# Hybrid encoder layer: the MLP in two phases, with the down projection as seven half-size products

## The chip, the cores and the metric

The kernel runs on one NeuronCore of a Trainium2 chip. The metric is the device time of one execution in microseconds. The kernel before took 2099.94 us, the median of three runs (2098.85 to 2100.46). Its profile comes from one more execution, which has a time of its own (below).

All data are float32. TensorE gets every large operand as two parts of the type fp32r, a high part and the rest, and adds three matmuls (high x high, high x low, low x high), so that close to float32 accuracy is kept.

## The reference

One layer on 512 tokens of width 2048. Two mixers read the normalised input, their outputs are projected and added to the residual, then comes a gated MLP of width 5632 with a convolution of width 3 over the tokens, and a last RMS norm:

```python
proj = jnp.einsum("bsd,dc->bsc", rms_norm(x, attn_norm_g), w_in)      # 2048 -> 5120
y_conv = conformer_conv(u_val, u_gate, ...)                           # first two column blocks
y_na = neighborhood_attention(q, k, v, rpb)                           # other three column blocks
mixed = jnp.concatenate([rms_norm(y_conv, conv_out_g), rms_norm(y_na, na_out_g)], axis=-1)
x = x + jnp.einsum("bsc,cd->bsd", mixed, w_out)                       # 2048 -> 2048
up = jnp.einsum("bsd,df->bsf", rms_norm(x, ffn_norm_g), w_up)         # 2048 -> 2 x 5632
up = depthwise_conv(up, ffn_dw_w, ffn_dw_b)                           # width 3, over tokens
gate, val = jnp.split(up, 2, axis=-1)
x = x + jnp.einsum("bsf,fd->bsd", jax.nn.silu(gate) * val, w_down)    # 5632 -> 2048
return rms_norm(x, final_norm_g)
```

The change concerns the MLP and the last norm, and what the stages ahead of them carry for these two.

## The kernel before

**Layout.** Activations are held with channels on the 128 partitions and the 512 tokens along the free axis: 16 tiles for the width of 2048 (KD), 44 for the hidden width (NF). Weights come from DRAM in units of 128 x 1024 (512 KB), eight 128 x 128 blocks each. A block is stationary in TensorE and an activation tile moves past it.

**The weight pipeline.** `raw_unit` (L103) loads a unit on SP's queue into one of 7 raw buffers (NR). `parts` (L107) splits it: ACT writes the high part `whi` (L110), VectorE the low part `wlo` (L111), each in one of 4 buffers (NW). `plan` lists in order how every unit of the program is made, and `weights()` (L142) hands out the next one. Each call first makes the units up to 3 places ahead (AHEAD), so that their loads and splits stand in the engines' queues before the matmuls that use them; and it starts the entries of `sums` up to 8 places ahead (FAR). `mm3` (L118 to L123) issues the three matmuls of a block: L121 high x high, L122 high weight x low activation, L123 low weight x high activation. `tick` lets statistics and attention steps advance between units.

**The stages.** The projections, with convolution and attention beside them, run to about 500 us. The output projection follows in two halves (`out_half`, L461), the convolution group's to about 612 us, the attention group's to about 699 us. `after` (L501) closes each of the 16 column tiles of the second half: it adds the product to the residual x2 (L503), writes the sum to DRAM (`xd`), adds its squares, and for each pair of tiles makes seven combinations for the up projection.

**The up projection.** It is done by the Strassen-Winograd scheme: the 2 x 2 block product (a pair of width tiles by two halves of 256 tokens; gate and value columns) needs seven products of half the size in place of eight. The activations' seven combinations are made once (`comb`, through `halves`, L494 to L499: a split of 128 x 256 by ACT L497 and VectorE L498). The weights' combinations are made anew for each of the 44 hidden tiles in `factors` (L535): the quarters A22, A11 and A12 are used as they are, the sums A22 + A21 and A21 + A11 are made by an accumulating DMA of POOL's queue on a raw buffer (L543), the other two by VectorE adds (L554, L560). `up` (L597) runs the products in the order 0 to 6, each of 8 blocks x 3 matmuls, 256 wide; it copies products 0, 1 and 3 out of PSUM by ACT and joins the rest by VectorE adds. `hidden` (L641) multiplies gate and value by the norm's factor (L643, L644), convolves each (`conv3`: ACT L635, VectorE L636 and L637), and forms silu(gate) x value (L646, L647).

**The down projection** runs beside it, a chunk of 4 hidden tiles (CH) behind: 11 chunks (NCH). When a chunk's four tiles are made, `in_two` splits them. While the next chunk's up products run, `down` (L656) issues 4 x 3 matmuls, 512 wide, for each of the 16 output tiles, copies the result out of PSUM (L665), and adds it to the residual in DRAM with an accumulating DMA on POOL's queue (L666). `down_units` sets after which up products this happens. At the last chunk the residual is loaded back, and the last down products run in two halves of 256 tokens (L700 to L712). Each half's norm takes the sum of squares over the partitions by matmuls (L177, L193), and `finish` (L696) applies norm and gain (L697) and writes the output, channel tile by channel tile (L698). The host transposes it.

**What orders the work.** Every engine, and each DMA queue (SP's and POOL's), runs its instructions in the order in which the program emits them, with few exceptions (`issue_after`, `keep_in_program_order`, `shifted`). An instruction that waits holds up all that stand behind it in its queue.

Of the kernel before, what the change touches and what calls it, by code (L numbers as in the profile page):

```python
# [16 lines left out]
P = 128  # L17
# [17 lines left out]
U = 8  # L35
# [6 lines left out]
CH = 4  # L42
NCH = NF // CH
# [6 lines left out]

ORDER = "aaaqqaqaaaqqaqqq"
# [4 lines left out]
         ("nag", NC_), ("g2", KD), ("fww", 2 * NF * 3), ("fwb", 2 * NF), ("g3", KD)]  # L56
# [9 lines left out]
def layer(ctx: ExitStack, tc: tile.TileContext, xT, w_in, w_out, w_up, w_down, par, tab, out):  # L66
# [51 lines left out]
    def mm3(ps, w, wk, mh, ml, start, stop):  # L118
        hi, lo = w[:2]
        a = slice(wk * P, (wk + 1) * P)  # L120
        nc.tensor.matmul(ps, hi[:, a], mh, start=start, stop=False)  # L121
        nc.tensor.matmul(ps, hi[:, a], ml, start=False, stop=False)  # L122
        return nc.tensor.matmul(ps, lo[:, a], mh, start=False, stop=stop)  # L123
# [18 lines left out]
    def weights():  # L142
        at = weights.at
        weights.at += 1
        for i in range(at, min(at + 1 + FAR, len(plan))):
            sum_ = sums.pop(i, None)
            if sum_ is not None:
                sum_()
# [3 lines left out]

    sums = {}

    weights.at = 0
# [94 lines left out]
    def project(n):  # L250
        ps = psm.tile([P, S], F32, tag="mm", name="pj")
        for u in range(KD // U):
# [4 lines left out]
            tick(m)  # L257
            while late:
                late.pop()()
# [201 lines left out]
    def out_half(m, read):  # L461
        for d in range(KD):
# [4 lines left out]
            tick(i)  # L467
            read(d, ps)
# [22 lines left out]
    xd = [dram.tile([P, S], F32, name=f"x2d{d}") for d in range(KD)]  # L491
# [8 lines left out]

    def after(d, ps):  # L501

        nc.vector.tensor_add(x2[d], x2[d], ps)  # L503
        nc.sync.dma_start(xd[d], x2[d])
        sum_sq(acc2, x2[d], d == 0)
        if d % 2 == 0:
            return
# [14 lines left out]
        for c, f in enumerate((t4_, t1, t3, b11, t2_, b21, b22)):  # L522
            halves(f, c)
# [11 lines left out]
    def factors(f):  # L535
# [5 lines left out]
        def summed(q1, q2):  # L541
            t = load(q1)
            nc.gpsimd.dma_start(t, w_up[f, q2], accum_op=ALU.add)  # L543
            return t

        def make(c):
            if c == 0:
                return load(A22)
            if c == 1:
                return a["s"]  # L550
            elif c == 2:
                return a[A21]
            elif c == 3:
                return load(A11)  # L554
            elif c == 4:
                add(a["s"], a["s"], a[A11])
            elif c == 5:
                return load(A12)
            else:
                add(a["s"], a["s"], a[A12])  # L560
            return a["s"]

        a = {}

        def ahead(c):
# [211 lines left out]
```

## Time and profile before

| | before |
|---|---|
| median of three runs | 2099.94 us (2098.85 to 2100.46) |
| the profiled execution's own time | 2099.91 us |
| its span, first to last instruction | 2098.1 us |
| matmuls / TensorE's mean granted clock | 13024 / 0.995 of full speed |
| moved by DMA | 340 MB, on average 162 GB/s |

How to read it. The page gives each engine's busy time as a share of the span: PE is TensorE's matmuls, PEld its loading of stationary blocks (which overlaps them), DVE is VectorE, ACT is ScalarE, POOL is GpSimd, SP is SyncE, which here only issues DMAs. A group row reads: line, engine, operation, output <- inputs, shapes and types, x count | busy us, mean ns of one | idle time of the engine just before them and what ended most of it. A timeline row reads: start, duration, engine, line, operation, shapes, x count, and in brackets the idle time before it and what released it. A window row reads: stretch, length, busy us and instruction count of PE, PEld, DVE, ACT and POOL in this order, then TensorE's granted clock, the busy share of the DMA engines, and GB/s. Matmuls overlap in the pipeline, so the busy time of one is longer than the distance from one to the next.

### The profile page before, as it was taken

The page shows a single profiled execution, that of the slowest core. Times are in us where ns is not written, and L with a number is a line of the kernel's source. Part 1 is how long each engine was busy: PE and PEld are TensorE (multiplying, and loading weights), DVE is VectorE, ACT ScalarE, POOL GpSimd, SP SyncE. Part 2 cuts the span into 40 slices and gives each one's busy share as a digit, 9 for nine tenths or more (in the row PEclk, how much of TensorE's full clock was granted, in tenths as well). Part 3 has the DMA queues.
Part 4 walks back from the last instruction along what each step waited for, and adds up shares of the span by engine and source line. Part 5 has one row for each costly group of instructions (what it writes and reads, how often), then busy time and mean ns, then how long its engine had stood idle before and what let it go on. Part 6 is the DMA issues. An engine that isn't in the chain of part 4 may idle for free.

```text
span 2098.1 us, 32752 instructions
## 1 busy us (share of the span) xinstructions
PE 2064.4 (98%) x13024; PEld 1851.4 (88%) x13024; DVE 1485.3 (71%) x2049; ACT 990.9 (47%) x1472; POOL 217.8 (10%) x254
## 2 busy tenths in 40 slices
PE   8999999999999999999999999999999999999997
PEld 6888888877878899999999999999999999999987
DVE  7986796686568887766766767666676675767667
ACT  6144424457436545444544544454454544545452
POOL 0000000000000001111121111111111111111110
PEclk9999999999999999999999999999999999999998
DMA  6232222235325567777787787787787777777772
GB/s 227 85 126 101 91 90 101 101 102 208 113 91 173 146 177 181 188 195 177 181 198 182 185 195 177 190 190 184 183 196 181 177 195 192 174 188 189 169 203 81
DMA packets 114921, 340.13 MB, mean 162 GB/s; under 512 B 12752, under 2 KB 16848, under 8 KB 114768
## 3 DMA queue, kind: packets, MB, share of 16 engines
q1 hardware_dynamic: 79056, 249.95, 35.7%
q0 software_dynamic: 35712, 88.10, 24.9%
q8 instruction: 102, 1.67, 0.3%
q14 instruction: 51, 0.42, 0.1%
HBM read 287.66 MB, written 50.33 MB: 161 GB/s over the span
## 4 chain that ended last, share of the span: by engine, by line
PE 96%; DVE 2%; ACT 1%; DMA 1%; issue 0%; SPq 0%; DVEq 0%; ACTq 0%
PE pu L121 14%; PE pu L123 14%; PE pu L122 14%; PE pd L121 8%; PE pd L122 8%; PE pd L123 8%; PE pj L121 7%; PE pj L123 7%; PE pj L122 7%; PE po L121 3%; PE po L122 3%; PE po L123 3%; PE sc L373 1%; PE po L416 1%; PE trp L403 1%; DMA raw<-in_w_in 1%
## 5 line engine op out<-in xcount | busy, mean ns | idle before, releaser
L111 DVE TENSOR_TENSOR wlo<-raw,whi 128x1024 fp32r<-128x1024 f32 x500 | 610.2, 1221 | 455.8 <-ACT whi L110 429.6
L110 ACT ACTIVATE whi<-raw 128x1024 fp32r<-128x1024 f32 x500 | 529.3, 1060 | 835.5 <-PE pu L122 302.0
L121 PE MATMUL pu<-xc,whi 128*128 128x256 f32 x2464 | 699.0, 284 | 2.4 <-ACT whi L110 2.4
L122 PE MATMUL pu<-xc,whi 128*128 128x256 f32 x2464 | 697.5, 283 | 0.0
L123 PE MATMUL pu<-xc,wlo 128*128 128x256 f32 x2464 | 697.3, 283 | 0.0
L121 PEld LDWEIGHTS pu<-xc,whi 128*128 128x128 f32 x2464 | 472.9, 192 | 9.2 <-ACT vv L618 2.7
L122 PEld LDWEIGHTS pu<-xc,whi 128*128 128x128 f32 x2464 | 473.1, 192 | 3.6 <-issue 0.5
L123 PEld LDWEIGHTS pu<-xc,wlo 128*128 128x128 f32 x2464 | 472.8, 192 | 0.0
L121 PE MATMUL pj<-xh,whi 128*128 128x512 f32 x640 | 253.5, 397 | 7.7 <-ACT whi L110 7.7
L121 PE MATMUL pd<-hh,whi 128*128 128x512 f32 x640 | 250.2, 391 | 1.9 <-ACT pdc L665 1.9
L123 PE MATMUL pj<-xh,wlo 128*128 128x512 f32 x640 | 250.1, 391 | 1.2 <-DVE wlo L111 1.2
L122 PE MATMUL pj<-xl,whi 128*128 128x512 f32 x640 | 250.8, 392 | 0.0
L122 PE MATMUL pd<-hl,whi 128*128 128x512 f32 x640 | 250.0, 391 | 0.0
L123 PE MATMUL pd<-hh,wlo 128*128 128x512 f32 x640 | 249.0, 389 | 0.0
L666 POOL DMA_DIRECT2D x2d<-pdc x160 | 140.5, 880 | 776.4 <-ACT pdc L665 744.5
L543 POOL DMA_DIRECT2D raw<-in_w_up x88 | 77.7, 883 | 1040.4 <-DVE xc L498 637.9
L287 DVE SCALAR_TENSOR_TENSOR y<-ch,prm,y 128x507 f32<-128x507 f32 (+14 forms) x240 | 169.9, 738 | 3.1
L665 ACT ACTIVATE pdc<-pd 128x512 f32<-128x512 f32 x160 | 94.1, 589 | 136.6 <-PE pd L123 136.6
L121 PEld LDWEIGHTS pj<-xh,whi 128*128 128x128 f32 x640 | 120.6, 188 | 36.2 <-ACT whi L110 9.0
L123 PEld LDWEIGHTS pj<-xh,wlo 128*128 128x128 f32 x640 | 120.5, 188 | 28.3 <-DVE wlo L111 2.7
L123 PEld LDWEIGHTS pd<-hh,wlo 128*128 128x128 f32 x640 | 120.2, 188 | 25.7
L121 PEld LDWEIGHTS pd<-hh,whi 128*128 128x128 f32 x640 | 120.5, 188 | 24.9 <-ACT pdc L665 2.3
(138 smaller groups left out, 2224.7 us busy)
## 6 DMA issues: line engine op xcount, KB each, us to landing
raw<-in_w_up SPq DMA_DIRECT2D x220, 512.0 KB, 4.0
raw<-in_w_up POOLq DMA_DIRECT2D x88, 512.0 KB, 5.5
raw<-in_w_down SPq DMA_DIRECT2D x88, 512.0 KB, 3.7
raw<-in_w_in SPq DMA_DIRECT2D x80, 512.0 KB, 3.6
x2d<-pdc POOLq DMA_DIRECT2D x160, 256.0 KB, 5.5
raw<-in_w_out SPq DMA_DIRECT2D x32, 512.0 KB, 3.3
x<-in_xT SPq DMA_DIRECT2D x32, 256.0 KB, 6.0
tab<-in_tab SPq DMA_DIRECT2D x32, 256.0 KB, 4.0
```

The lines of the kernel that those rows point to most:

```text
L110: i = nc.scalar.activation(hi[:, :n], raw[:, :n], AF.Copy)
L111: j = nc.vector.tensor_sub(lo[:, :n], raw[:, :n], hi[:, :n].bitcast(F32))
L121: nc.tensor.matmul(ps, hi[:, a], mh, start=start, stop=False)
L122: nc.tensor.matmul(ps, hi[:, a], ml, start=False, stop=False)
L123: return nc.tensor.matmul(ps, lo[:, a], mh, start=False, stop=stop)
L287: nc.vector.scalar_tensor_tensor(y[:, a:b], h[:, a + j - PAD:b + j - PAD], prm[:, o + j:o + j + 1], y[:, a:b], op0=ALU.mult, op1=ALU.add)
L373: m = nc.tensor.matmul(both[:, j, i, :], q[hp, b * P:(b + 1) * P], grid(k, KC0[b], KW)[hp], start=True, stop=True)
L403: m = nc.tensor.transpose(ps[:, 2 * i + ch, :], s[:, i, ch * P:(ch + 1) * P], ident)
L416: m = nc.tensor.matmul(grid(po, b * BLK, BLK)[hp], vt[b // 2][:, 2 * (b % 2) + ch, hp], pts[j][:, 2 * i + ch, :], start=(ch == 0), stop=(c ...
L543: nc.gpsimd.dma_start(t, w_up[f, q2], accum_op=ALU.add)
L665: nc.scalar.activation(t, ps, AF.Copy)
L666: nc.gpsimd.dma_start(xd[d], t, accum_op=ALU.add)
```

## The change

The MLP becomes two phases. First all 44 up tiles are made; then the down projection is done whole.

**Up phase.** The order of the seven products is TURN. Products 4 and 2 are accumulated on the PSUM tile of product 3, product 6 on that of product 1, so that the running sums of the scheme are formed by TensorE in PSUM and read out after each step (`kept`, `add`). The accumulating flags need `mm3`'s new argument `more`. Finished hidden tiles 0 to 35 are written to DRAM (`hd`) by SP's queue, the last 8 (KEEP) stay on chip. In the last up tile `again` issues the 36 reloads.

**Weight sums of the down projection.** The host cuts w_down into 22 pairs of hidden tiles (NK) by four quarters of 128 x 1024. Of the seven weight factors three are quarters; the other four (`wsum` 1, 2, 4, 6) are built in DRAM by `sum_ahead`: a DMA copies a quarter or an earlier sum to the DRAM tile, a second one accumulates another quarter on it, both on POOL's queue, behind a matmul that `behind` names. Of these 88 jobs 50 are issued in the projections, 16 in the first and second half of the output projection, and 22 after the fourth product of up tiles 0 to 21.

**Down phase.** Activations are stationary (128 x 128), weights move (512 wide), and the result has tokens on the partitions. The order of the products is TURN2, each over all 22 pairs, the 4 pairs kept on chip first (`order2`). `operand` forms the activations' combination for a pair and splits it; `product2` issues 4 output tiles (2 token tiles x 2 column tiles) x 3 matmuls a pair. Its last 3 pairs (TAIL) run tile by tile, so that the four PSUM tiles end one after another. Products 4 and 2 accumulate on the PSUM tiles of product 3, product 6 on those of product 1. `onto` adds a PSUM tile to a quarter of the residual.

**Residual and last norm.** `turned` transposes each residual tile on TensorE (four 128 x 128 transposes), copies it out of PSUM on ACT, with the sign that the scheme wants, and writes it to DRAM with tokens on the rows (`xt`); `rest` loads it back in the down phase. `ready` squares and sums a finished piece by ACT and multiplies it by the gain, which comes as a table of its own (`g3`, 128 x 2048); `write` forms the factor per token and scales and writes the pieces, the second token half first. The output is (512, 2048), and the host doesn't transpose it.

```diff
+TURN = (3, 0, 1, 4, 5, 2, 6)
+TURN2 = (3, 0, 4, 1, 2, 6, 5)
+Q = D // 2 // S
+TAIL = 3
+ROW = 2048
...
+    def behind(i, ins):
+        tc.add_manual_dep(i.ins, ins.ins.name,
+                          mybir.DependencyInfo(mybir.DependencyClass.Sync, mybir.DependencyReason.DATA),
+                          reason="behind")
+
+    def sum_ahead(ins):
+
+        if not jobs:
+            return
+        c, k = jobs.pop(0)
+        a, b = {1: (w_down[k, A22], A21), 2: (w_down[k, A21], A11), 4: (wsum[1][k], A11), 6: (wsum[4][k], A12)}[c]
+        behind(nc.gpsimd.dma_start(wsum[c][k], a), ins)
+        nc.gpsimd.dma_start(wsum[c][k], w_down[k, b], accum_op=ALU.add, max_dma_last_dim=ROW)
...
+    def turned(d):
+
+        ps = psa.tile([P, S // P, P], F32, tag="tr", name="trx", bufs=2)
+        for t in range(S // P):
+            nc.tensor.transpose(ps[:, t, :], x2[d][:, t * P:(t + 1) * P], ident)
+        r = t2("xt").rearrange("p (t k) -> p t k", t=S // P)
+        nc.scalar.activation(r, ps, AF.Copy, scale=1.0 if d < KD // 2 else -1.0)
+        o = d % (S // P) * P
+        for t in range(S // P):
+            nc.sync.dma_start(xt[t][d * P // S][:, o:o + P], r[:, t, :])
...
         nc.vector.tensor_add(x2[d], x2[d], ps)
-        nc.sync.dma_start(xd[d], x2[d])
         sum_sq(acc2, x2[d], d == 0)
+        turned(d)
...
+        for c, qs in ((1, (A22, A21)), (2, (A21, A11))):
+            sums[at + TURN.index(c)] = lambda c=c, qs=qs: summed("s%d" % c, *qs)
+        return [lambda c=c: parts(make(c), U * P)[:2] for c in TURN]
...
+    order2 = [*range(NK - KEEP // 2, NK), *range(NK - KEEP // 2)]
+    for c in TURN2:
+        for k in order2:
+            plan.append(lambda c=c, k=k: unit(wsum[c][k] if c in wsum else w_down[k, {0: A22, 3: A11, 5: A12}[c]],
+                                              U * P))
...
+        a = kept(uu[:, 0], product(3))
+        kept(vv[:, 0], product(0))
+        b = kept(vv[:, 1], product(1))
+        kept(uu[:, 1], product(4, a))
+        add(g[:, 0], uu[:, 0], product(5))
+        add(v, vv, both(product(2, a)))
+        add(g[:, 1], uu[:, 1], product(6, b))
...
         nc.vector.tensor_mul(g, g, v)
-        return g
...
+        if f < NF - KEEP:
+            nc.sync.dma_start(hd[f], g)
+        else:
+            hs[f] = g
+
+    back = [f for p in range(2) for f in range(p, NF - KEEP, 2)]
+
+    def again(at, i):
+        for _ in range(8):
+            if back:
+                f = back.pop(0)
+                hs[f] = t2("h")
+                behind(nc.sync.dma_start(hs[f], hd[f]), i)
+
+    def paced(at, i):
+        if at == 3:
+            sum_ahead(i)
+
+    for f in range(NF):
+        hidden(f, again if f == NF - 1 else paced)
...
+    def operand(c, k):
...
+        t = t2("ho", F32R)
+        nc.scalar.activation(t[:, :H], src, AF.Copy)
+        nc.vector.tensor_sub(t[:, H:], src, t[:, :H].bitcast(F32))
+        return t
...
+            nc.tensor.matmul(ps[i], h[:, t], wh[:, d], start=start and not more, stop=False, skip_group_check=more)
+            nc.tensor.matmul(ps[i], h[:, t], wl[:, d], start=False, stop=False, skip_group_check=more)
+            nc.tensor.matmul(ps[i], h[:, tl], wh[:, d], start=False, stop=stop, skip_group_check=more)
+
+        n = NK - TAIL
+        for j, k in enumerate(order2[:n]):
+            w, h = weights(), operand(c, k)
+            for i in range(2 * Q):
+                feed(w, h, i, j == 0, False)
+        got = [(weights(), operand(c, k)) for k in order2[n:]]
+        for i in range(2 * Q):
+            for j, (w, h) in enumerate(got):
+                feed(w, h, i, False, j == TAIL - 1)
...
+            q = t2("sq")
+            nc.scalar.activation(q, y[i], AF.Square, accum_out=sq[th][:, t, d:d + 1])
+            nc.vector.tensor_mul(y[i], y[i], gs[d])
...
+    a = four(True)
+    product2(3, a, False)
+    e3 = onto(rest(0, 0), a)
+    b = four(False)
+    product2(0, b, False)
+    e0 = onto(rest(0, 1), b)
+    product2(4, a, True)
+    e4 = onto(rest(1, 0), a)
+    b = four(False)
+    product2(1, b, False)
+    e1 = onto(rest(1, 1), b)
+    product2(2, a, True)
+    for y, th in ((e0, 0), (e1, 1)):
+        ready(onto(y, a), th, 1)
+    product2(6, b, True)
+    ready(onto(e4, b), 1, 0)
+    a = four(True)
+    write(1, (e4, e1))
+    product2(5, a, False)
+    ready(onto(e3, a), 0, 0)
+    write(0, (e3, e0))
```

274 lines of the change are left out of this document (131 added, 143 removed).

## The prediction

> **What bounds the kernel now.** I read the page's busy times and its chain of waits first, then the groups of instructions by line, then the timeline and the windows of single stages.
>
> ```profile
> span 2098.1 us, 32752 instructions
> PE 2064.4 (98%) x13024; PEld 1851.4 (88%) x13024; DVE 1485.3 (71%) x2049; ACT 990.9 (47%) x1472; POOL 217.8 (10%) x254
> PE 96%; DVE 2%; ACT 1%; DMA 1%; issue 0%; SPq 0%; DVEq 0%; ACTq 0%
> ```
>
> The chain that ends last is 96% TensorE, so time is matmuls times their pitch, plus the places where TensorE waits. A matmul's mean duration isn't its pitch, because matmuls overlap. The pitch is the distance of start times in the timeline:
>
> ```profile
> 689.82 0.39 PE L121 MATMUL po<-mbh,whi 128*128 128x512 f32 x1
> ...
> 698.66 0.39 PE L121 MATMUL po<-mbh,whi 128*128 128x512 f32 x1
> 739.82 0.28 PE L121 MATMUL pu<-xc,whi 128*128 128x256 f32 x1
> ...
> 748.82 0.28 PE L121 MATMUL pu<-xc,whi 128*128 128x256 f32 x1
> ```
>
> L121 is the first of each group of three. Thirteen groups in 8.84 us give 0.2267 us for a matmul 512 wide, 25 groups in 9.00 us give 0.120 us for one 256 wide.
>
> **What is removed and added on TensorE.**
>
> ```profile
> L121 PE MATMUL pd<-hh,whi 128*128 128x512 f32 x640 | 250.2, 391 | 1.9 <-ACT pdc L665 1.9
> L121 PE MATMUL pd<-hh,dh 128*128 128x256 f32 x128 | 36.7, 287 | 1.2 <-ACT dh L693 1.2
> 136.65 1.02 PE trp L403 x8
> ```
>
> Lines 122 and 123 have the same counts. The down projection is now 1920 x 0.2267 + 384 x 0.120 = 481.4 us. After, it is 22 pairs of hidden tiles x 7 products x 4 output tiles x 3 = 1848 matmuls, all 512 wide with a 128x128 stationary: 418.9 us, 62.4 less. The up projection keeps its 7392 matmuls; collecting products 4, 2 and 6 in PSUM takes adds from VectorE, not matmuls. The 16 x 4 transposes of the residual are new. Eight such transposes take 1.02 us in the chain, so 64 take 8.2 us. They stand between matmuls of the next unit, after the add that they need, and wait for nothing.
>
> In the last chunk, TensorE waited while residual tiles and accumulations shared the DMA engines:
>
> ```profile
> 2010.00:2015.00 5.00, 4.81 (x22) 3.64 (x20) 5.00 (x8) 3.62 (x7) 0.00 (x0) 1.00 0.71 225
> 2015.00:2020.00 5.00, 3.28 (x14) 2.72 (x15) 2.33 (x4) 2.22 (x5) 1.77 (x2) 1.00 1.03 373
> 2030.00:2035.00 5.00, 3.79 (x17) 2.74 (x15) 0.46 (x1) 2.20 (x5) 1.47 (x2) 1.00 0.99 191
> ```
>
> 0.19 + 1.72 + 1.21 = 3.1 us idle. That stage goes.
>
> **Up phase: VectorE and DMA.**
>
> ```profile
> L111 DVE TENSOR_TENSOR wlo<-raw,whi 128x1024 fp32r<-128x1024 f32 x500 | 610.2, 1221 | 455.8 <-ACT whi L110 429.6
> L637 DVE SCALAR_TENSOR_TENSOR uy<-g,prm,uy 128x511 f32<-128x511 f32 x44 | 32.8, 745 | 0.0
> L643 DVE TENSOR_TENSOR g<-g,rstd 128x512 f32<-128x512 f32 x44 | 30.5, 692 | 1.5
> L498 DVE TENSOR_TENSOR xc<-t,xc 128x256 fp32r<-128x256 f32 x32 | 12.1, 420 | 3.4 <-ACT xc L497 3.4
> 750.00:800.00 50.00, 50.00 (x410) 49.58 (x409) 44.56 (x56) 26.39 (x37) 3.48 (x4) 1.00 0.60 167
> ```
>
> An up tile alone lasts 168 x 0.120 = 20.2 us. VectorE does 9 operations of 1.22, 4 of 0.75, 4 of 0.69 and 2 of 0.42 us in it, 17.6 us, 87%. From 750 to 800, before any down unit runs, VectorE was 89% busy and TensorE lost nothing, so I cost this at nothing; without that slack a tile would take as long as VectorE does.
>
> The new transfers are 88 sums in DRAM (a copy of 0.52 MB, then an accumulate of 0.52 MB), 36 hidden tiles of 0.26 MB written and read back, and 160 accumulations of 0.26 MB that go. Sixty-six sums run before the up phase, where the page shows the DMA engines two to five tenths busy; 22 run one per up tile in tiles 0 to 21. Prices, from one view of the DMA queues by stretch each (750 to 800, 2015 to 2040, 0 to 30):
>
> ```profile
> DMA  6232222235325567777787787787787777777772
> ...
> q1 hardware_dynamic: 1706, 6.19, 35.8%
> q0 software_dynamic: 576, 2.10, 24.3%
> q0 software_dynamic: 1152, 2.10, 54.0%
> q1 hardware_dynamic: 3888, 9.79, 88.1%
> raw<-in_w_up POOLq DMA_DIRECT2D x88, 512.0 KB, 5.5
> ```
>
> A load moves 6.19 MB in 17.9 us, 346 GB/s (371 when saturated); an accumulate into SBUF 173 GB/s, into DRAM 155 GB/s. An up tile then needs 7.6 us for five loads, 6.1 for two accumulates, 0.8 for the hidden tile, 1.5 + 3.4 for the sum: 19.4 of 20.2 us. No row shows a transfer from DRAM to DRAM. Its pair costs at least 2.8 us (both halves at 371 GB/s), or twice 4.9 if DRAM is charged for reading and writing. I take 4.9, the sum of the nearest rows, and no stall: seven raw buffers put each load some 14 us or more ahead of its use, and the accumulate lands in 5.5 us.
>
> POOL's queue is in order: behind a sum's copy, which waits for the tile's fourth product, stand the up accumulates of the tile after next, due over 20 us later. On SP's queue each hidden tile's write waits for VectorE with the next raw loads behind it, which have the same lead.
>
> **Joins of the down phase.** Durations for what follows:
>
> ```profile
> L635 ACT ACTIVATE uy<-g,prm 128x512 f32<-128x512 f32 x44 | 35.4, 805 | 2.1 <-DVE g L643 2.1
> L646 ACT ACTIVATE uy<-uy 128x512 f32<-128x512 f32 x44 | 27.8, 632 | 6.9 <-DVE uy L637 2.7
> L497 ACT ACTIVATE xc<-t 128x256 fp32r<-128x256 f32 x32 | 11.5, 406 | 13.9 <-DVE t L521 13.9
> L169 ACT ACTIVATE sq<-x 128x512 f32<-128x512 f32 x30 | 17.3, 620 | 1.8 <-DVE x L503 1.8
> L388 ACT ACTIVATION_READ_ACCUMULATOR s<-s,nm 128x1 f32 x64 | 12.0, 187 | 0.0
> L110 ACT ACTIVATE whi<-raw 128x1024 fp32r<-128x1024 f32 x500 | 529.3, 1060 | 835.5 <-PE pu L122 302.0
> ```
>
> Here the order of VectorE's queue decides. In all three places TensorE's next product needs a small split of activations (ACT 0.41 us, VectorE 0.42 us) that stands behind the arithmetic of the product just finished.
>
> Up to down: the fourth down unit reuses the weight buffer of the last up product (NW = 4), and its split is queued before tile 43's arithmetic. From the end of that product: split 1.06 + 1.22, two adds of 0.42 and one of 0.69, two multiplies of 0.69, the first convolution on ACT 0.8, four steps of 0.75, the last multiply 0.69, the activation split 0.42, and 0.6 for hand-overs: 10.5 us. Two matmuls can run before the low part is needed, so 10.0 us idle.
>
> Product 2 to product 6: TAIL lets the four PSUM tiles finish 6.1, 4.1, 2.0 and 0 us before the end. VectorE has eight adds and eight multiplies of 0.69 and three weight splits queued before product 6's first activation split. Two of the splits wait for buffers until 1.4 and 0.7 us before the end, on ACT too. Four adds and two multiplies are done by then; what is left is 2 x 1.22 from -0.2, ten of 0.69 with ACT's six squares of 0.81 between them, a split 1.22 and 0.42: +10.7, so 10.3 us idle.
>
> Product 6 to product 5: half as many (four adds, four multiplies). Left are two splits from -0.2, an add, a multiply, a split, a multiply, a small reduction and 0.42: +6.2, so 5.7 us idle.
>
> The other three joins have activation splits made ahead. Only product 0's operands strain VectorE: 1.22 + 2 x 0.42 + 2 x 0.47 = 3.0 us a unit against TensorE's 2.72, started during product 3. Thirteen units make 3.6 us of lag at a point with 2 us of slack; I take 2 us (0 to 4).
>
> What follows a long wait:
>
> ```profile
> 593.14 0.77 PE L121 MATMUL po<-mah,whi 128*128 128x512 f32 x1 [3.54 <-DVE oa L483]
> ...
> 598.40 0.63 PE L121 MATMUL po<-mah,whi 128*128 128x512 f32 x1
> 593.00:599.00 6.00, 5.86 (x14) 4.63 (x15) 3.09 (x5) 0.00 (x0) 0.00 (x0) 0.50 0.20 76
> ```
>
> After 3.5 us idle the granted clock is 0.50, and 12 matmuls take 5.26 us, 0.44 each. With the thirteenth, that loses 2.7 us. Three joins: 8.1 us. The Trainium skill, "TensorE: Matmul & The Clock Gate", section "What's actually happening", has the array at half clock after about 3.4 us idle and at full clock again after about 3.4 us of work. By that a restart would cost half of 3.4, an estimate of 1.7 us, and the sum would be 3 us less; the trace shows a longer half-clock stretch.
>
> Reload at the first join: 36 tiles, 9.4 MB, go out on SP's queue in order from 17 us before the up phase ends, with the fifth weight unit behind them and a table of the final gain (on which VectorE waits) behind that. At 371 GB/s all that is on chip some 15 us after the end, and the fifth unit split at 22; TensorE asks for it at 10.0 + 2.7 + 4 x 2.72 = 23.6. Hidden, by the join's own wait; without that it would be 12 us late.
>
> **Tail.**
>
> ```profile
> 2082.25 0.28 PE L123 MATMUL pd<-hh,dl 128*128 128x256 f32 x1
> ...
> 2084.01 0.60 PE L177 MATMUL st<-ones,acc 128*128 128x1 f32 x4 [1.48 <-DVE acc L170]
> 2084.65 0.16 DVE L180 TENSOR_SCALAR rsv<-st 128x2 f32<-128x2 f32 x1 [0.70 <-PE st L177]
> 2086.07 0.48 DVE L190 TENSOR_SCALAR dg<-ident,rsy 128x128 f32<-128x128 f32 x2
> 2087.47 6.36 DVE L697 SCALAR_TENSOR_TENSOR x<-x,prm,st 128x256 f32<-128x256 f32 x16 [0.92 <-PE st L193]
> L511 ACT ACTIVATE b<-x,prm 128x512 f32<-128x512 f32 x16 | 10.6, 710 | 0.0
> ```
>
> The last product ends at 2082.5, the span 15.6 us later, 4.3 of them after the last instruction of L697. After: add, square, multiply 2.4, eight small steps 1.8, four scalings on ACT 2.8, the same 4.3: 11.4. Gain 4.2.
>
> **Sum.** 2098.1 - 62.4 + 8.2 - 3.1 + 26.0 + 8.1 + 2 - 4.2 = 2072.7 us of span, plus 1.8 around it (2099.91 less 2098.1): 2074. The profiled execution is 0.03 us from the median, so this is the median too.
>
> **Rivals.**
> - DMA takes over (the other side). The up tiles 0 to 21 need 19.4 of 20.2 us of the DMA engines at my price. From 0.8 us more they are the bound, and from 2 us more (a DRAM pair of 6.9 us) the change is slower than before. At twice my price a tile takes 24.3 us: 22 x 4.1 = 90, 2164 us. For: the 99% busy stretch around 2020, where accumulates moved 155 GB/s. Against: saturated loads go faster than in the price.
> - The reload is late. At 250 GB/s the 9.4 MB take 12 us longer, nothing hides them: 2086. For: 256 KB pieces, eight in flight. Against: the first 30 us, where such pieces went at 371.
> - The joins are covered, because VectorE gets ahead: 2074 - 26 - 8 = 2040. Against: its queue is in order, and the rows price what stands before the splits.
>
> **How the numbers follow.** Forecast 0.60 (2074; its own range 2064 to 2086), late reload 0.17, DMA-bound 0.17 (2100 upward), covered joins 0.06. The range 2056 to 2112 takes in the late reload and the mild part of the DMA case. A measurement here can tell 0.2%, 4 us. Faster: 0.60 + 0.06 + most of the late reload, less what I may have missed, 0.76; slower 0.19; same 0.05.
>
> **What would show it.** TensorE idle of about 10, 10 and 6 us at the start of the first, sixth and seventh down product, each released by ACT or VectorE of the split, with a clock of 0.5 behind it; elsewhere a pitch of 0.2267 us; up tiles every 20.2 us with tiles 0 to 21 no longer than the rest. Longer early up tiles with the DMA engines full would mean the first rival; a wait for the fifth unit's load the second.

## The result and the profile after

The changed kernel takes 2067.16 us, the median of four runs (2062.83 to 2071.45), against 2099.39 (2096.79 to 2100.46) for the kernel before. The ratio is 0.9848, with a 95% interval of 0.9825 to 0.9872. The forecast was 2074 us in a range of 2056 to 2112, so the time lies 7 us below the forecast and within the range. Single executions of the changed kernel differ by 8.6 us, so this closeness says little by itself; the terms are compared one by one below. The profiled execution of the changed kernel took 2068.41 us, with a span of 2066.6.

From the profile page after: the span, the engines' busy times, the chain that ended last, and two groups of TensorE.

```profile
span 2066.6 us, 32277 instructions
PE 2011.7 (97%) x12620; PEld 1799.9 (87%) x12620; DVE 1588.8 (77%) x2201; ACT 1019.7 (49%) x1548; POOL 202.8 (10%) x270
PE 91%; DVE 4%; DMA 2%; ACT 1%; issue 1%; SPq 0%; ACTq 0%; DVEq 0%
L728 PE MATMUL pd<-whi,ho 128*128 128x512 f32 x616 | 242.6, 394 | 19.6 <-ACT ho L708 19.6
```

The matmuls fell by 404, from 13024 to 12620. TensorE's share of the chain fell from 96% to 91%. The chain follows whatever released each step, so the 5% of difference is not all idle time of TensorE. Idle time that the change brought stands in the last row: 19.6 us in front of the down products, ended by the small activation split (`ho`) on ACT.

Stage borders come from the first start of each group. These are the rows of before, then of after, from the view of one source line (name, count, shortest/median/longest ns, first to last start):

```profile
L121 PE MATMUL pu<-xc,whi x2464: 277/283/1202, 699.3 to 2008.8; 128*128 128x256 f32 x190
...
L121 PE MATMUL po<-mah,whi x128: 387/389/799, 500.0 to 611.6; 128*128 128x512 f32 x128
L121 PE MATMUL po<-mbh,whi x128: 389/389/389, 612.3 to 698.7; 128*128 128x512 f32 x128
L121 PE MATMUL pd<-hh,dh x128: 278/283/467, 2034.6 to 2082.0; 128*128 128x256 f32 x128
```

```profile
L126 PE MATMUL pu<-xc,whi x2464: 278/283/387, 716.8 to 1607.7; 128*128 128x256 f32 x190
...
L126 PE MATMUL po<-mah,whi x128: 387/389/799, 503.0 to 620.0; 128*128 128x512 f32 x128
L126 PE MATMUL po<-mbh,whi x128: 387/389/397, 620.7 to 716.1; 128*128 128x512 f32 x128
...
L728 PE MATMUL pd<-whi,ho x616: 389/389/797, 1617.0 to 2052.9; 128*128 128x512 f32 x154
...
L730 PE MATMUL pd<-whi,ho x616: 387/389/794, 1618.0 to 2053.3; 128*128 128x512 f32 x154
```

| us of the span | before | after | difference |
|---|---|---|---|
| projections and first half of the output projection | 612.3 | 620.7 | +8.4 |
| second half of the output projection | 87.0 | 96.1 | +9.1 |
| up and down, matmuls at their pitch | 1368.4 | 1305.9 | -62.5 |
| up and down, all that TensorE lost in it | 14.7 | 30.9 | +16.2 |
| after the last product | 15.7 | 13.1 | -2.6 |
| span | 2098.1 | 2066.6 | -31.5 |

The third row is 887.0 us of up matmuls (7392 x 0.120) plus 481.4 before and 418.9 after. The fourth row is the length of the stage less that. A join is here the passage from one product's work to the next product, and the half clock is a stretch in which the granted clock is 0.50. Of the 30.9 us after, 4.3 were lost in the up phase, 20.1 waiting at the three joins, and 6.5 to the half clock behind them.

### The profile page after: what moved, and what is told of

It reads as the page before. It is cut to its first block, busy times and chain, and to the rows that moved or that the text cites. A ratio compares the mean times of both kernels' runs of the same rounds, so it can differ in the third digit from the quotient of the medians.

```text
span 2066.6 us, 32277 instructions
## 1 busy us (share of the span) xinstructions
PE 2011.7 (97%) x12620; PEld 1799.9 (87%) x12620; DVE 1588.8 (77%) x2201; ACT 1019.7 (49%) x1548; POOL 202.8 (10%) x270
## 4 chain that ended last, share of the span: by engine, by line
PE 91%; DVE 4%; DMA 2%; ACT 1%; issue 1%; SPq 0%; ACTq 0%; DVEq 0%
PE pu L126 14%; PE pu L127 14%; PE pu L128 14%; PE pd L728 7%; PE pd L729 7%; PE pd L730 7%; PE pj L126 6%; PE pj L128 5%; PE pj L127 5%; PE po L126 3%; PE po L127 3%; PE po L128 3%; DMA tab<-in_tab 2%; DVE y L311 1%; DVE wlo L116 1%
## 5 line engine op out<-in xcount | busy, mean ns | idle before, releaser
L115 ACT ACTIVATE whi<-raw 128x1024 fp32r<-128x1024 f32 x574 | 605.1, 1057 | 824.9 <-PE pj L127 216.3
L116 DVE TENSOR_TENSOR wlo<-raw,whi 128x1024 fp32r<-128x1024 f32 x574 | 700.6, 1223 | 283.0 <-ACT whi L115 247.6
L728 PE MATMUL pd<-whi,ho 128*128 128x512 f32 x616 | 242.6, 394 | 19.6 <-ACT ho L708 19.6
L729 PE MATMUL pd<-wlo,ho 128*128 128x512 f32 x616 | 242.0, 393 | 0.0
L730 PE MATMUL pd<-whi,ho 128*128 128x512 f32 x616 | 241.2, 393 | 0.0
L728 PEld LDWEIGHTS pd<-whi,ho 128*128 128x128 f32 x616 | 117.2, 190 | 44.9 <-ACT ho L708 20.7
L127 PEld LDWEIGHTS pj<-xl,whi 128*128 128x128 f32 x640 | 120.6, 188 | 24.4 <-issue 0.7
L730 PEld LDWEIGHTS pd<-whi,ho 128*128 128x128 f32 x616 | 116.7, 190 | 25.3 <-DVE ho L709 1.1
L729 PEld LDWEIGHTS pd<-wlo,ho 128*128 128x128 f32 x616 | 117.1, 190 | 24.3
L177 POOL DMA_DIRECT2D ws<-in_w_down x88 | 79.1, 899 | 483.2 <-DMA ws<-in_w_down 270.8
```

What stands on the lines that cost most here:

```text
L115: i = nc.scalar.activation(hi[:, :n], raw[:, :n], AF.Copy)
L116: j = nc.vector.tensor_sub(lo[:, :n], raw[:, :n], hi[:, :n].bitcast(F32))
L127: nc.tensor.matmul(ps, hi[:, a], ml, start=False, stop=False, skip_group_check=more)
L177: nc.gpsimd.dma_start(wsum[c][k], w_down[k, b], accum_op=ALU.add, max_dma_last_dim=ROW)
L728: nc.tensor.matmul(ps[i], h[:, t], wh[:, d], start=start and not more, stop=False, skip_group_check=more)
L729: nc.tensor.matmul(ps[i], h[:, t], wl[:, d], start=False, stop=False, skip_group_check=more)
```

## The joins, as they came out

The timeline of after around the three waits. The first row is the last up matmul; of the others the PE rows are the first matmuls of products 3, 6 and 5.

```profile
1607.96 0.28 PE L128 MATMUL pu<-xc,wlo 128*128 128x256 f32 x1
...
1616.03 0.63 ACT L664 ACTIVATE uy<-uy 128x512 f32<-128x512 f32 x1 [1.54 <-DVE uy L652]
1616.57 1.32 ACT L708 ACTIVATE ho<-uy 128x256 fp32r<-128x256 f32 x4
1616.70 0.69 DVE L665 TENSOR_TENSOR uy<-uy 128x512 f32<-128x512 f32 x1
1617.02 0.80 PE L728 MATMUL pd<-whi,ho 128*128 128x512 f32 x1 [8.78 <-ACT ho L708]
...
1921.46 1.88 DVE L754 TENSOR_TENSOR xr<-xr,pd 128x512 f32<-128x512 f32 x3
...
1925.06 2.49 DVE L774 TENSOR_TENSOR xr<-xr,g 128x512 f32<-128x512 f32 x4
1925.87 1.32 ACT L708 ACTIVATE ho<-uy 128x256 fp32r<-128x256 f32 x4
1926.32 0.80 PE L728 MATMUL pd<-whi,ho 128*128 128x512 f32 x1 [6.96 <-ACT ho L708]
...
1928.60 1.43 DVE L709 TENSOR_TENSOR ho<-uy,ho 128x256 fp32r<-128x256 f32 x4
...
1992.29 0.80 PE L728 MATMUL pd<-whi,ho 128*128 128x512 f32 x1 [3.90 <-ACT ho L708]
```

At each join TensorE waits for `ho`, a split of 0.41 us whose input has long been there. It waits because `ho` stands in its engine's queue behind the arithmetic of the work just finished. The brackets count from the modelled end of a matmul. Counted from the pitch, the first matmul is late by 1617.02 - 1608.08 = 8.9 us, then by 7.1 and 4.1.

## The experiments

The runs are told by subject, not by number. All times below are single profiled executions beside the changed kernel's span of 2066.6 us, but for the kernel of run 8, which was timed in five rounds. The first stage's length varies between kernels that are alike up to there, so stages are compared, not only spans.

**1. Activation splits ahead.** A list keeps the operands of the next three pairs made, across the borders of products:

```diff
-            w, h = weights(), operand(c, k)
+            (h,), w = operands(1), weights()
...
-        got = [(weights(), operand(c, k)) for k in order2[n:]]
+        ops = operands(TAIL)
+        got = [(weights(), o) for o in ops]
```

> The down phase's activation splits are issued three pairs ahead of their use, also across the border of two products; nothing else is moved. In the changed kernel TensorE idled 8.9, 7.1 and 4.1 us at the starts of the first, sixth and seventh product, and lost 3.0, 2.1 and 1.4 us to the half clock after them. Theory 1 (mine: the split stands behind the arithmetic in VectorE's queue): the sixth and seventh product start at once; what is left is a wait at their fourth unit, whose weight split still stands behind the arithmetic, of at most some 3 us each, so the span falls by 8 to 13 us from 2066.6; the first join stays, because there the splits are still issued after tile 43's arithmetic. Theory 2 (the wait is for weight splits or PSUM, not for the small split): the idle time at the two starts stays above 4 and 2 us.

Measured: span 2050.0. TensorE's waits, from the view of waits (total, times, longest):

```profile
PE pd L739 <- ACT ho L692: 8.8, 1, 8.8
...
PE pd L740 <- DVE wlo L116: 0.7, 1, 0.7
```

The wait of 8.8 us is the first join, which this run leaves. The waits at the sixth and seventh product are gone but for the 0.7 us for a weight split, 0.9 by the pitch. The down phase, from the first to the last matmul, is 422.9 us, where the changed kernel took 436.5. So the position of the small split was the cause, not the amount of arithmetic. What is left, 0.9 us, is less than the 3 us allowed for.

**2. The first join.** In addition, the operands of four pairs are made in the middle of tile 43, that tile's gate arithmetic runs inside product 3, and the odd hidden tiles are reloaded there:

```diff
+        if f == NF - 1:
+            todo.append(lambda m: gate(f, g, v))
...
+        if at == 2:
+            operands(0, 4)
...
+            if len(back) > (NF - KEEP) // 2:
+                reload(i)
...
+    todo.extend([lambda m: (reload(m), reload(m))] * ((NF - KEEP) // 4))
...
+            if j >= 1 and todo:
+                todo.pop(0)(m)
```

> As the run before, and at the first join the splits of the first four pairs are issued in the middle of the last up tile, the last tile's gate arithmetic is issued after the second unit of product 3, and the reloads of the odd hidden tiles go out two per unit in product 3. Theory 1: TensorE goes from the up phase into product 3 without a wait and stays at full clock, 11.9 us less than the run before (8.9 idle, 3.0 half clock). Theory 2 (the reload is what TensorE waits for next, as one rival had it): a wait of 3 to 12 us at the fifth unit, where the first reloaded tile or the weights behind the reloads on SP's queue are needed.

Measured: span 2041.7. Two windows at the join (length, then PE, PEld, DVE, ACT, POOL, clock, DMA share, GB/s):

```profile
1600.00:1608.00 8.00, 8.00 (x67) 7.83 (x66) 6.10 (x10) 4.80 (x10) 0.00 (x0) 1.00 1.04 388
1608.00:1616.00 8.00, 8.00 (x38) 6.61 (x37) 7.76 (x13) 5.83 (x8) 0.00 (x0) 1.00 0.84 331
```

TensorE is busy throughout and the clock stays at 1.00. Up to the last matmul, the join and the down phase together are 420.6 us, where the first run had 8.9 + 422.9 = 431.8: 11.2 less, against 11.9 expected.

**3. The arithmetic spread.** As the first, and each piece (add, square, multiply) of products 2 and 6 is issued behind a unit of the next product:

```diff
-    for y, th in ((e0, 0), (e1, 1)):
-        ready(onto(y, a), th, 1)
+    for i in range(2 * Q):
+        for y, th in ((e0, 0), (e1, 1)):
+            todo.append(lambda m, y=y, a=a, th=th, i=i: piece(y, a, th, 1, i))
...
```

> As the first of these runs, and the adds, squares and gain multiplies of products 2 and 6 are issued one piece per unit of the following product, not all before it. Theory 1: no wait over 0.5 us at the sixth and seventh product or at their fourth units, all 14.6 us of idle and half clock there are gone, span about 2052, with the first join unchanged. Theory 2 (the arithmetic as such is too much for VectorE): it comes back as waits of several us in products 6 and 5, because a unit there has 1.22 + 0.42 + 1.38 us of VectorE work against 2.72 us of TensorE.

Measured: span 2052.2, down phase 421.1 us, with no wait but the first join's. Behind that join the clock is at half for the first nine matmuls:

```profile
1618.10:1622.00 3.90, 3.90 (x9) 3.00 (x10) 1.65 (x5) 3.90 (x14) 0.00 (x0) 0.50 1.04 402
1622.10:1626.00 3.90, 3.90 (x19) 3.21 (x18) 1.01 (x3) 3.69 (x10) 0.00 (x0) 1.00 1.05 404
```

They take 4.0 us where 9 x 0.2267 is 2.0, so 2.0 us are lost there and 419.1 us are left for the matmuls. Nothing else is lost, and VectorE keeps up. Against the first run this stage gains 1.8 us: 0.9 are its last wait, and 0.9 come from the half clock, which cost the first run 2.9 us behind the same wait. The first stage, 4 us longer, hides this in the span (below).

**4. Bias tables one step earlier** in the attention:

```diff
-        yield
-        scores(0)
+        tbs = load(0)
+        yield
+        scores(0, tbs)
+        tbs = load(2)
         yield
         yield
-        scores(2)
+        scores(2, tbs)
```

> In the attention the bias tables are loaded one step earlier; nothing else is moved from the changed kernel. In the changed kernel the projections end 3.0 us later than before (first output-projection matmul 503.0, was 500.0) and the first half of the output projection takes 117.7 us, was 112.3. Theory 1 (the DRAM sums share the DMA engines, so the tables land late, and VectorE with TensorE behind it waits for them): both go back to within 1 us of before, 8 us less. Theory 2 (the sums slow the weight loads as well): at least half of the 8.4 us stays, with TensorE waiting for weight splits.

In the changed kernel the tables are late. From the view of the tile, what VectorE waited for, the two kernels one after the other, before and after:

```profile
  DMA tab<-in_tab: 2.3, 3
...
DMA to landing us min/median/max: 3.4/4.0/8.3
```

```profile
  DMA tab<-in_tab: 21.2, 11
...
  PE sc L397: 4.1, 1
...
DMA to landing us min/median/max: 4.2/6.2/13.3
```

Measured: VectorE's waits for tables fall to 5.9 us, where the six other runs with the changed kernel's first stage (1, 2, 3, 6, 7 and 10) have 16.1 to 24.2. One wait of TensorE of 3.8 us stays, again for a table. So the late tables are one cause, as in theory 1, but the remedy is not complete. The second half of the output projection starts at 615.5, not 620.7. That does not show a gain in time, since run 7, with the first stage of the changed kernel, got there at 615.5 as well. The projections do not go back to their old length either: the output projection starts at 509.2, because loading earlier moved attention work from one stage to the other. The two borders have to be taken together.

**5. No DRAM sums in the projections**; 28 of them in the down phase:

```diff
-            if weights.at > 6 and weights.at % 3:
-                sum_ahead(m)
...
+            if j % 3 == 2:
+                sum_ahead(m)
```

> The changed kernel without DRAM sums in the projections: 16 sums in the output projection, one in each of the 44 up tiles, the other 28 in the down phase, one for every three units, in an order that makes each sum before its product. Theory 1 (the early sums are what delays the attention): the second half of the output projection starts at 612 to 613 us (before 612.3, changed kernel 620.7), the up phase keeps its 891 us, the down phase its 436.5, span about 2058. Theory 2 (the time only moves): the sums in the down phase delay weight units there, since a sum takes the DMA engines some 4.3 us (0.94 less 0.73 of a tile of 20.26 us) and the weights of three units use about 4.2 of 8.2 us; the down phase gets 3 us longer or more.

```profile
L126 PE MATMUL po<-mbh,whi x128: 387/389/397, 610.9 to 706.3; 128*128 128x512 f32 x128
```

Span 2057.8. The second half of the output projection starts at 610.9, 1.4 us earlier than in the kernel before and 4.6 earlier than in any run that keeps the sums of the projections as they were, and VectorE waits 2.9 us for tables. So the sums in the projections are the whole cause of the 8.4 us. One sum in each of 44 tiles leaves the up phase at 891.3 us, and the down phase is 437.6, 1.1 longer than with the sums made early.

**6. Two sums a tile in tiles 0 to 10**, not one in tiles 0 to 21:

```diff
-        if at == 3:
+        if at in (1, 4):
             sum_ahead(i)
```

> The changed kernel with the 22 sums of the up phase two per tile in tiles 0 to 10, not one per tile in tiles 0 to 21. By the changed kernel's shares a tile without a sum uses the DMA engines 0.73 x 20.26 = 14.8 us and a sum adds 4.3, so two make 23.4. Theory 1 (the DMA engines bind once their work exceeds the tile): tiles 0 to 10 take some 3 us more each, 25 to 35 us in all, with weights late. Theory 2 (the order on POOL's queue binds: each sum's second transfer waits there some 7 us for its first, with the up phase's accumulates behind it): longer than that, over 40 us, with waits for the summed weights. Theory 3 (seven buffers and faster transfers take it up): under 5 us.

Measured: up phase 922.2 us, 30.9 more than in the changed kernel, span 2097.2: all but 0.9 us of the gain is lost. That is the number of theory 1, but the share of the DMA engines isn't. Windows of the changed kernel in tiles with and without a sum, then of this one:

```profile
920.00:1180.00 260.00, 260.00 (x2169) 260.00 (x2168) 216.37 (x246) 135.80 (x182) 41.13 (x51) 1.00 0.93 248
1180.00:1500.00 320.00, 320.00 (x2669) 320.00 (x2668) 266.42 (x303) 166.50 (x224) 26.94 (x31) 1.00 0.73 194
```

```profile
715.00:935.00 220.00, 205.84 (x1651) 203.09 (x1649) 161.82 (x199) 104.85 (x149) 40.59 (x54) 0.98 0.93 250
```

Twice the sums a tile, yet the same 0.93 and 250 GB/s: the engines did no more. The views of waits of POOL and ACT from 720 to 960 show where the time went:

```profile
POOL ws L177 <- DMA ws<-in_w_down: 77.5, 10, 11.3
POOL ws L177 <- DMA ws<-ws: 45.9, 10, 5.4
POOL raw L580 <- issue: 30.7, 7, 8.5
```

```profile
ACT whi L115 <- DMA raw<-in_w_up: 43.3, 5, 10.9
```

Of 240 us, 123 are waits of a sum's second transfer for its first. The up phase's accumulates (L580) come behind them, ready but not issued, and ACT's weight splits, which TensorE needs, wait up to 10.9 us for them. So the next run separates the two.

**9. The same bytes, the queue freed.** Each sum's accumulate is issued at the next step, beside the next sum's copy, and the sums are taken in an order in which none needs the one just ahead:

```diff
-    jobs = [(c, k) for k in range(NK) for c in (1, 4, 2, 6)]
+    jobs = [(c, k) for n in range(0, NK, 2) for c in (1, 4, 2, 6) for k in (n, n + 1)]
...
+        if begun:
+            c, k, b = begun.pop()
+            behind(nc.gpsimd.dma_start(wsum[c][k], w_down[k, b], accum_op=ALU.add, max_dma_last_dim=ROW), ins)
...
         behind(nc.gpsimd.dma_start(wsum[c][k], a), ins)
-        nc.gpsimd.dma_start(wsum[c][k], w_down[k, b], accum_op=ALU.add, max_dma_last_dim=ROW)
+        begun.append((c, k, b))
```

> The kernel with two sums per tile in tiles 0 to 10 again (up phase 922.2 us, 30.9 more than the changed kernel), now with each sum's second transfer issued one step later, beside the next sum's copy, in an order in which no transfer needs the one just ahead of it. The bytes per tile are the same. Theory 1 (the DMA engines bind): the up phase stays over 915 us. Theory 2 (POOL's queue binds, where each accumulate waits 5 to 8 us for its copy with the up phase's accumulates behind it; the share of the DMA engines was 0.93 in both kernels): the up phase goes back to 891 to 896 us.

```profile
715.00:935.00 220.00, 218.70 (x1814) 217.60 (x1814) 180.53 (x219) 116.82 (x163) 47.06 (x61) 1.00 1.02 279
```

```profile
POOL ws L175 <- DMA ws<-ws: 50.7, 9, 7.8
POOL ws L175 <- DMA ws<-in_w_down: 45.0, 7, 8.9
```

Up phase 891.4 us, with the DMA engines at 1.02 and 279 GB/s. Theory 2 holds: in run 6 it was the order on POOL's queue, not the engines, that made TensorE wait. The queue isn't free of waits: its accumulates into DRAM (L175) still wait 96 us for copies in the same stretch. But the up accumulates no longer stand ready behind them: their time of that kind falls from 30.7 to 1.6 us.

**7. The old joining of the up products** by VectorE's adds, in the old order:

```diff
-TURN = (3, 0, 1, 4, 5, 2, 6)
+TURN = (0, 1, 2, 3, 4, 5, 6)
...
-        a = kept(uu[:, 0], product(3))
-        kept(vv[:, 0], product(0))
-        b = kept(vv[:, 1], product(1))
-        kept(uu[:, 1], product(4, a))
-        add(g[:, 0], uu[:, 0], product(5))
-        add(v, vv, both(product(2, a)))
-        add(g[:, 1], uu[:, 1], product(6, b))
...
+        for i in range(2):
+            nc.scalar.activation(vv[:, i], product(i), AF.Copy)
...
+        add(v, vv, both(product(2)))
+        nc.scalar.activation(u, product(3), AF.Copy)
+        add(u2, u, product(4))
+        add(v, v, both(u2))
+        add(vv[:, 1], vv[:, 1], u2)
+        add(g[:, 0], u, product(5))
+        add(g[:, 1], vv[:, 1], product(6))
```

> The changed kernel with the up products in the old order and their results joined by VectorE as before, not in PSUM: two more adds of 256 columns and one of 512 a tile, 1.5 us of VectorE. Theory 1 (VectorE has slack in the up phase): the up phase stays at 891 us within 2 us. Theory 2 (VectorE is near enough to its limit to hold TensorE up): 0.5 us a tile or more, over 20 us in all.

Windows from 900 to 1500, of the changed kernel and of this one:

```profile
900.00:1500.00 600.00, 600.00 (x5003) 600.00 (x5002) 499.36 (x568) 312.62 (x419) 71.27 (x86) 1.00 0.82 219
```

```profile
900.00:1500.00 600.00, 600.00 (x5002) 600.00 (x5001) 524.72 (x655) 309.63 (x388) 70.75 (x86) 1.00 0.83 219
```

VectorE goes from 83% to 87%, and TensorE is busy throughout in both. The up phase is 896.7 us, 5.4 more than in the changed kernel, outside the 2 us of theory 1: the loss is at its two ends, 2.4 us in one wait in the first tile (1.5 in the changed kernel) and 4.3 in two waits in the last. Within the phase, collecting in PSUM is worth nothing. Whether the 5.4 us come from the adds or from the order of the products, which changed with them, was not separated.

**10. All reloads in the last up tile**, with the first join mended as in the second run. The edit is shown against that run:

```diff
-            if len(back) > (NF - KEEP) // 2:
+            if back:
                 reload(i)
...
-    todo.extend([lambda m: (reload(m), reload(m))] * ((NF - KEEP) // 4))
```

> The kernel with the first join mended (TensorE goes on without a wait), but with all 36 reloads issued in the last up tile, as in the changed kernel. The sixth weight unit of the down phase and the table of the gain stand behind all 36 on SP's queue. Theory 1 (my step: hidden by the join's own wait, late without it): TensorE waits 4 to 12 us in the first eight units of product 3, for weight splits. Theory 2 (the transfers are faster than I took them): no wait over 0.5 us, span as with the odd reloads later, 2041.7 within 3.

The view of waits from 1600 to 1660:

```profile
DVE g L787 <- DMA g<-in_g: 4.9, 1, 4.9
...
PE pd L750 <- ACT whi L115: 4.2, 1, 4.2
```

Span 2049.2. In this stretch TensorE waits once, from 1622.1, 4.4 us for a weight split, and is at half clock behind it; the down phase is 427.0 us, 6.4 more than in the second run. So the first join's wait hid the reload: a kernel that mends the join and leaves the reload keeps 4.8 of the 11.2 us (431.8 less 427.0).

**8. Everything together**, and no sums after the 60th weight unit of the projections:

```diff
-            if weights.at > 6 and weights.at % 3:
+            if 6 < weights.at < 60 and weights.at % 3:
```

> All three joins mended (the kernel of the second run and that of the third together), bias tables one step earlier, and no sums after the 60th weight unit of the projections (14 sums move to up tiles 22 to 35). Theory 1: the sum of the parts, 11.9 for the first join, 14.6 for the other two, 6 to 8 for the attention: a span of 2032 to 2035, 3.1 to 3.2% below before. Theory 2 (the parts share a resource and give some of it back): over 2040.

Measured in five rounds: 2033.18 us (2032.17 to 2034.11), ratio to before 0.9689, interval 0.9676 to 0.9702. In the profiled execution:

```profile
span 2030.4 us, 32267 instructions
```

The gains add up, with a span 1.6 us below the expected 2032 to 2035: the second half of the output projection starts at 610.4, the up phase takes 891.5 us, there is no wait at the first join, and the down phase takes 419.1.

## Why the prediction was right, point by point

**The matmuls.** Gain forecast 62.4, and the runs bear it out: freed of waits, the 1848 matmuls took 419.1 us (in the third run less its half clock, and in the eighth as it stands), 418.9 forecast. So the pitch with activations stationary, 0.2268 us, is the pitch with weights stationary.

**The transposes.** Forecast 8.2, measured 9.1 (96.1 less 87.0). No wait came with them.

**VectorE and the DMA in the up phase.** Costed at nothing, rightly: tiles of 20.26 us, 44 in 891.3 us, those with a sum no longer than the rest. A sum in DRAM takes (0.93 - 0.73) x 20.26 = 4.1 us of the engines, 4.9 taken. The rival "DMA takes over" did not come, and it had the wrong mechanism. Two sums per tile cost 30.9 us in the sixth run, near what the DMA engines' shares had given for them (25 to 35), but the ninth run moved the same bytes with no such wait. What was near its limit is POOL's queue, which the prediction saw ("behind a sum's copy ... stand the up accumulates") and took to be clear, the accumulates being due over 20 us later; at twice the sums it was not clear.

**The joins.** Place and releaser were right in all three, a small split of activations behind the arithmetic of the work just finished, and runs 1 and 2 show it. The sizes were 10.0, 10.3 and 5.7, and measured 8.9, 7.1 and 4.1. At the first join the terms listed add up to 10.7, not 10.5, and the last two were not on the path: ACT's split (1616.57) released TensorE before VectorE's last multiply (1616.70) was done. At the sixth product the step that failed is "a split 1.22 and 0.42" after the last multiply: the matmuls that need only the high part went first. Six of them stand before the first L730, so ACT's split released TensorE, and VectorE's share (L709 at 1928.60) came later, at no cost. The ten operations were also charged at 0.69 each; in a row they take 2.49 / 4 = 0.62.

**What follows a wait.** 8.1 forecast, 3.0 + 2.1 + 1.4 = 6.5 measured. The three differ because the half clock ends at times of its own, not a fixed while after a restart (last section): behind the same first wait it cost 2.0 us in the third run. The prediction's estimate of 1.7 us a restart, from the Trainium skill, "TensorE: Matmul & The Clock Gate", section "What's actually happening", gives 5.1 us for three, also an estimate. The measured time lies between that and the forecast.

**The reload.** Forecast: hidden by the join's own wait, 12 us late without it. By the prediction's own numbers it is 11 (a split at 22, asked for at 4 x 2.72). The tenth run shows both the hiding and a lateness of 4.4 us. There the late unit was the sixth, not the fifth, which is asked for 2.7 us later. Its load went out at 1618.7, behind the last reload and the gain table, and its split ended 18 us after the last up matmul, not 22; the DMA engines moved 387 to 395 GB/s from 1600 to 1624, not 371.

**Product 0's strain on VectorE.** 2 us forecast, none found: the joins and the half clock account for all that the down phase took above its matmuls (436.5 - 418.9 = 17.6, and 7.1 + 4.1 + 6.5 = 17.7).

**The tail.** Gain of 4.2 forecast, 2.6 measured. The step "the same 4.3" after the last scaling failed: from the end of the last scaling (2060.63) to the end of the span it is 6.0 us. Eight stores of 256 KB are issued one after another, until 2063.1, where the old ones were half as large.

```profile
2058.07 2.56 ACT L793 ACTIVATE xr<-xr,rsy 128x512 f32<-128x512 f32 x4 [1.02 <-DVE rsy L785]
...
2058.59 4.47 SPq L795 DMA_DIRECT2D out_T<-xr  x8
```

**Two terms that were missing.** The sums in the projections were costed at nothing because the DMA engines were two to five tenths busy there. That step was wrong: a mean share says nothing of when the tables of the attention come. VectorE waited 21.2 us for these in place of 2.3, and the stage became 8.4 us longer (run 5; 3 to 9 us by execution, as the last section's 615.5 to 621.7 against 612.3). On the other side, the kernel before lost 14.7 us in up and down together, where the prediction counted only the 3.1 us of the last chunk. Against the pitch, its start to 740 us lost 6.3, the chunks to 2010 us 3.0, and the last chunk 5.3. The window of its start, beside that of after:

```profile
699.30:740.00 40.70, 38.27 (x298) 36.75 (x298) 31.96 (x52) 22.05 (x34) 3.12 (x4) 0.96 0.58 161
```

```profile
716.80:760.00 43.20, 41.90 (x340) 40.79 (x339) 32.94 (x52) 25.04 (x39) 6.21 (x9) 1.00 0.85 221
```

With 4.3 us lost in the up phase after, that is 10.4 gained, 7.3 more than forecast. That the two omissions nearly cancel (8.4 against 7.3) is luck. The forecast was 6.1 us of span too high mainly because the joins (5.9) and the half clock (1.6) were over-priced and the lag of product 0 (2.0) was not there; the transposes and the tail took 2.5 back, and the two omissions 1.1.

## What to carry to other kernels

Where one product follows another, look at which small operation TensorE needs next and what stands ahead of it in its engine's queue: issuing that operation three steps earlier gained 13.6 us here, and spreading the arithmetic as well only 0.9 more. A wait that is mended uncovers what it hid; here more than half of the first join's gain depended on moving the reload with it. A mean share of the DMA engines is no proof that a transfer is free: ask what small load is due in that stretch, and what stands behind a waiting transfer in its queue.

## What was not expected of the hardware

The half clock also came after waits shorter than the 3.5 us from which the prediction read it. In the sixth run TensorE's matmuls stop at 835.29 and go on at 837.68, 2.3 us late, and from 838.2 the granted clock is 0.50; after a wait of 2.7 us behind the matmul of 850.67 it stays at 1.00. Four windows of that run:

```profile
838.30:841.60 3.30, 3.30 (x18) 3.30 (x17) 1.97 (x3) 0.28 (x1) 0.00 (x0) 0.50 1.00 193
841.70:845.00 3.30, 3.30 (x29) 3.30 (x29) 1.38 (x2) 0.00 (x0) 0.00 (x0) 1.00 1.04 252
...
865.60:868.80 3.20, 3.20 (x18) 3.20 (x17) 1.50 (x3) 0.00 (x0) 0.45 (x1) 0.50 1.06 242
847.00:855.00 8.00, 5.42 (x45) 5.25 (x45) 4.21 (x5) 2.89 (x4) 1.44 (x2) 1.00 0.75 166
```

The stretches at half clock in this run's up phase start at 838.2, 865.5, 903.1, 950.9 and 995.2: the later four are 8, 19, 33 and 46 times 3.41 us after the first. The wait of 2.3 us lies whole in one step of this grid, 834.8 to 838.2; the one of 2.7 us is cut by a border at 851.9 into 1.1 and 1.7 us. The same section of the Trainium skill says that the window runs free, and this agrees; it also asks for an idle window, and here one that was idle for 2.2 or 2.3 of its 3.41 us was enough.

One wait shows it best. In all twelve kept traces TensorE waits 3.7 us by the pitch in the first half of the output projection, for VectorE's `oa`. Eleven of them have the half clock behind it. Run 7 does not: there a border at 597.3 cuts the wait, from 595.3 to 599.0, into 1.9 and 1.8 us. The window behind it:

```profile
599.10:602.40 3.30, 3.30 (x15) 2.71 (x16) 2.87 (x5) 0.00 (x0) 0.00 (x0) 1.00 0.84 240
```

So a wait of some 3 us may cost its own length only, or, as at 838.2, about 1.5 us more (16 matmuls at 0.213 us in place of 0.120), by where it falls. The share from which on a window counts as idle was not tried; in runs 6 and 7 a window idle for 1.9 us did nothing, and one idle for 2.1 us had the half clock behind it.

The changed kernel's time also spreads more than before's, 8.6 us against 3.7 over four runs each. In profiled executions of seven kernels with the same first stage (the changed kernel and runs 1, 2, 3, 6, 7 and 10), that stage ended between 615.5 and 621.7, and the kernel with fewer early sums and earlier tables spread by 1.9 us in five runs. That the tables' waits are the cause of the spread is only argued.
